# Seven products instead of eight in 34 more weight units, and one unit order on three engines

## The chip, the cores and the metric

One Trainium2 chip; the kernel uses one core of it. The metric is device time in microseconds (us) of one execution, lower is better. A profiled execution gives a trace: what every engine did and when. TensorE is written PE, VectorE DVE, ScalarE ACT, and the queue of SyncE, which issues nearly all transfers, SP.

## The reference

One block of a streaming encoder on x of 256 x 2048 (float32), with 2048-wide projections and a hidden size of 5632:

```python
x = x + 0.5 * swiglu(rms_norm(x, g1), w_gate, w_up, w_down)      # FFN 1: 2048 -> 5632 -> 2048
proj = rms_norm(x, g2) @ w_in                                    # 2048 -> 4112, split into u, q, k, v, g, a
y = concat(pool_mixer(u), gla_mixer(q, k, v, g, a))              # small mixers, 256 x 2048
x = x + y @ w_out
x = x + mem_cross_attention(rms_norm(x, g3), rms_norm(mem, g4))  # w_q, w_kv, 4 heads, w_o
x = x + 0.5 * swiglu(rms_norm(x, g5), w_gate2, w_up2, w_down2)   # FFN 2
out = rms_norm(x, g6)

def swiglu(h, w_gate, w_up, w_down):
    return (silu(h @ w_gate) * (h @ w_up)) @ w_down
```

With 256 rows against some 400 MB of weights the work is a long chain of matrix products in which each weight is used once.

## The kernel before

**Units.** All weights come as a stream of units of 1 MB, a tile `raw` of 128 x 2048 float32, in one order written out by the program (class `Stream`). A float32 product is made of three products in the fast float32 form: a weight is split into a high part `wh` (an ACT copy that rounds) and a low part `wl = raw - wh` (a DVE subtraction), activations are kept as a high and a low part too (`xs`, `ys`), and PE adds up high x high, high x low, low x high (`products`, line 291). While PE works on unit u, unit u+2 is split (`AHEAD = 2`, rings of three `wh` and `wl`) and unit u+5 is loaded (`RAW = 3`, a load is issued when the split that frees its tile is done). `Stream.emit` writes this out; `st.op(f, n)` puts other work n units later. The language then lets a scheduler choose each engine's order from a timing model of its own; every engine runs its queue in the order chosen.

**Groups.** A group is two or four 256 x 512 outputs summed over the depth. In `block_t` a unit holds two depth tiles (k) by 1024 columns: 24 matmuls of 512 columns. `block_a` (transposed outputs, line 276) and `block_b` serve the mixer and the attention and are not changed.

**Seven products.** `block_s` treats some units (`pairs`) as a 2 x 2 by 2 x 2 block product in the Strassen-Winograd form: seven products instead of eight, so 21 matmuls instead of 24 (`seven`, line 388). For that DVE makes four sums of the weight blocks (`add_weights`, lines 347 to 351, tile `T`), which are split like a weight (`split_seven`: `wh<-T`, `wl<-T`, and the three raw blocks that are used as they are, `xh`, `xl`). Sums of the activation blocks are made once by `part_sums` and kept in `xe`. A group with sevens needs four PSUM tiles of two banks each, which is all of PSUM: two hold parts (`a`, `b`) that belong to several outputs, two (`c`, `d`) hold the outputs themselves, on which the plain units (`unit_p`) add up as well. When the last seven is done, `combine` (lines 430 to 435) turns the parts into four tiles of corrections; at the group's end `join` (line 439) adds them to `c` and `d` and passes the sum to the group's own eviction.

Before the change sevens are used in 18 of the 20 gate and up groups of the two FFNs that are 1024 columns wide, in units 0, 2 and 4 of eight: 54 units. The first gate group of each FFN is a `block_t`.

**The order of the groups.** An FFN is cut into parts of 4, 4 and 3 blocks of 512 hidden columns. A part of 4 is gate, up, gate, up, then the down product in two groups of eight units (`into_x`, which adds the result to x rows fetched from and stored to memory). The part of 3 is gate, up, then one group `both` with 512 columns of gate and of up, then down in two groups of six units, in FFN 2 by `down_end`. The hidden activations reach `ys` through `turn` (PE transposes, line 678, then a split), one unit into the down product for those made last. `w_out` and `w_o` are two groups each through `into_x`. After the last down group, and after `w_out` and `w_o`, `fold` turns the new x into `xs`. `mem_in` and `mem_norm` (loading and normalising `mem`) lie in the `w_out` product.

Of the kernel before, what the change touches and what calls it, by code (L numbers as in the profile page):

```python
# [33 lines left out]
class Stream:  # L34
# [30 lines left out]
    def emit(self, load, prepare, split):  # L65
        done, w, late = -1, {}, []
        for u, f in self.items:
# [22 lines left out]
            f(*w.pop(u))  # L90


def build(ctx, tc, I, out):
# [122 lines left out]

    def split(hi, lo, src):
        nc.scalar.copy(hi, src)  # L218
        nc.vector.tensor_tensor(out=lo, in0=src, in1=f32(hi), op=ALU.subtract)  # L219
# [34 lines left out]
    def block_a(srcs, act, evict, delays=(0, 1)):  # L254
# [4 lines left out]
        def unit(gi):  # L259
            def fn(wh, wl):  # L260
# [3 lines left out]
                for kk in range(4):  # L264
# [3 lines left out]
                    for n in range(4):  # L268
# [6 lines left out]
                        for i, (o, w, x) in enumerate(parts):  # L275
                            nc.tensor.matmul(  # L276
                                o, w, x, start=k == 0 and i == 0, stop=last and i == 1
                            )
# [7 lines left out]
    def products(ps, act, k, h, wh, wl, first, last):  # L286

        tok = slice(h * P, (h + 1) * P)
        parts = [(act[:, k, 0, tok], wh), (act[:, k, 0, tok], wl), (act[:, k, 1, tok], wh)]
        for i, (a, w) in enumerate(parts):  # L290
            nc.tensor.matmul(ps, a, w, start=first and i == 0, stop=last and i == 2)  # L291
# [33 lines left out]
    def part_sums(act, ext, i, g):  # L325

        t = scope["pool"].tile([P, 4 * NB], F32, tag="T", name=uid("T"))
        a = t[:, :NB].rearrange("p (k s) -> p k s", k=2)
        e = t[:, NB : 2 * NB].rearrange("p (n s) -> p n s", n=4)
        nc.vector.tensor_tensor(  # L330
            out=a, in0=f32(act[:, 2 * g : 2 * g + 2, 0, :]), in1=f32(act[:, 2 * g : 2 * g + 2, 1, :]),
            op=ALU.add,
        )
        a11, a21, a12, a22 = (a[:, k, h * P : (h + 1) * P] for k in range(2) for h in range(2))
        nc.vector.tensor_tensor(out=e[:, 3], in0=a11, in1=a21, op=ALU.subtract)
        nc.vector.tensor_tensor(out=e[:, 1], in0=a22, in1=a21, op=ALU.subtract)
        nc.vector.scalar_tensor_tensor(
            out=e[:, 2], in0=e[:, 1], scalar=-1.0, in1=a11, op0=ALU.mult, op1=ALU.subtract
        )
        nc.vector.tensor_tensor(out=e[:, 0], in0=a12, in1=e[:, 2], op=ALU.add)  # L340
        split(ext[:, i, 0], ext[:, i, 1], e)
# [12 lines left out]
    def split_seven(u, raw, t):  # L354
# [4 lines left out]
        split(th, tl, t)  # L359
        parts = [x.rearrange("p (b n) -> p b n", n=NB) for x in (th, tl)]  # L360

        if True:
            r = [
                scope["pool"].tile([P, 3 * NB], F32R, tag=n, name=f"{n}{u}", bufs=2)
                for n in ("xh", "xl")
            ]
            split(*r, raw[:, NB:])
            parts.extend(x.rearrange("p (b n) -> p b n", n=NB) for x in r)
# [3 lines left out]
    def seven(banks, act, ext, i, g, first, later, weights):  # L372
# [3 lines left out]
        n4, n1, s2, s3 = ([ext[:, i, p, n] for p in range(2)] for n in range(4))  # L376
# [6 lines left out]
        order = ("P1", "P7", "P5", "P6", "P2", "P3", "P4") if first else (  # L383
            "P1", "P2", "P3", "P7", "P5", "P6", "P4")
        for n in order:
            (a, b), wh, wl = table[n]
            for j, (x, w) in enumerate(((a, wh), (a, wl), (b, wh))):
                nc.tensor.matmul(  # L388
                    banks[n], x, w, start=first and j == 0,
                    stop=not later and n in ("P1", "P5", "P6", "P7") and j == 2,  # L390
                )

    def block_s(srcs, act, ext, pairs, evict, delays=(0, 0)):

        held, n = {}, len(srcs)

        def open_banks():
            a, b, c, d = (ptile(uid("pt")) for _ in range(4))
            held["ps"] = (d, c)
            held["parts"] = (a, b)  # L400
            held["banks"] = {
                "P1": a[:, 0], "P6": a[:, 1], "P7": b[:, 0], "P5": b[:, 1],
                "P2": c[:, 0], "P4": c[:, 1], "P3": d[:, 0],
            }

        def unit_s(g):
            def fn(weights):
                if g == pairs[0]:
                    open_banks()
                seven(held["banks"], act, ext, pairs.index(g), g, g == pairs[0], g != pairs[-1],  # L410
                      weights)
            return fn

        def unit_p(g):
            def fn(wh, wl):
                wh, wl = (w.rearrange("p (k j n) -> p k j n", j=2, n=NB) for w in (wh, wl))
                for j in (1, 0):
                    for h in range(2):
                        for kk in range(2):

                            fresh = (j, h) == (0, 1) and g == min(set(range(n)) - set(pairs)) and kk == 0
                            products(held["ps"][j][:, h, :], act, 2 * g + kk, h, wh[:, kk, j],
                                     wl[:, kk, j], fresh, g == n - 1 and kk == 1)
            return fn

        def combine():
# [17 lines left out]
        for g, src in enumerate(srcs):  # L444
            if g in pairs:
                st.unit(src, unit_s(g), split_seven, add_weights)
                if g == pairs[-1]:
                    st.op(combine)
            else:
                st.unit(src, unit_p(g))  # L450
        for j in (1, 0):
            st.op(lambda j=j: join(j), delays[j])
# [138 lines left out]
    def residual(scale, b):  # L591

        def evict(j, ps):
# [4 lines left out]
            if j:  # L598
                store_x(b)
        return evict  # L600

# [15 lines left out]
    def into_x(w, act, scale, gain=None, k0=0, nk=KT, spread_too=True, src=None):  # L617
# [14 lines left out]
    PAIRS = (0, 2, 4)  # L632

    def pair_sums(g, delay):
        def f():
            if g == PAIRS[0]:
                rows["xe"] = scope["pool"].tile(
                    [P, len(PAIRS), 2, 4, P], F32R, tag="xe", name=uid("xe")
                )
            part_sums(xs, rows["xe"], PAIRS.index(g), g)  # L640
        st.op(f, delay)

    class Ext:


        def __getitem__(self, i):
            return rows["xe"][i]

    def ffn(wg, wu, wd, down):
        gate = {}  # L650

# [30 lines left out]

        for lo, n in FF_PARTS:
            for b in range(0, n - 1, 2):
                n0 = (lo + b) * NB
                if lo == b == 0:
                    block_t(wwide(wg, n0), xs, lambda j, ps: ev_gate(j, ps, 1))
                else:
                    block_s(wwide(wg, n0), xs, Ext(), PAIRS, lambda j, c: ev_gate(j, c, 0))
                block_s(wwide(wu, n0), xs, Ext(), PAIRS, ev_up)  # L690
                held = {}
                st.op(lambda held=held: held.update(gate))
                wait = PAIRS[-1] + 2 if b + 2 < n - 1 else 1
                for j in range(2):
                    st.op(lambda j=j, b=b, held=held: turn(held[j], 4 * (b + j)), wait)
            if n % 2:
                def both(j, ps):
                    if j:
                        ev_up(0, ps)
                    else:  # L700
                        ev_gate(0, ps, 1)
                block_t(wtwo(wg, wu, (lo + n - 1) * NB), xs, both)
                st.op(lambda n=n: turn(gate[0], 4 * (n - 1)), 1)
            down(wd, 4 * lo, 4 * n, lo + n == FF // NB)
# [10 lines left out]
    def down_first(wd, k0, nk, last):  # L715
        into_x(wd, ys, 0.5, G_MIX if last else None, k0, nk, src=None if k0 else I["x"][0])

    for g in PAIRS:
        pair_sums(g, 5)
# [577 lines left out]
```

## Time and profile before

| | |
|---|---|
| time of three runs | 2136.23, 2138.67, 2139.88 us, median 2138.67 us |
| the profiled execution | 2138.64 us |
| its span, first to last instruction | 2136.9 us; 1.7 us lie around it |
| mean granted TensorE clock | 0.998 |
| matmuls and weight loads on PE | 10032 each |
| moved by DMA | 435.92 MB, mean 204 GB/s |

A row of the groups names line, engine and operation, output<-inputs with their shapes, and how often; then total busy us and mean ns of one; then the idle time of the engine just before them and what ended it. PEld is the weight load, which runs beside the matmuls. The ends of matmuls are modelled and overlap, so the pace of matmuls is read from starts, not from their lengths.

### The profile page before, as it was taken

The numbers are of one execution on the slowest core, as the hardware profiler recorded it, in microseconds if no ns is written. First come the engines' busy times: TensorE is split into PE (matmuls) and PEld (weight loads), VectorE is DVE, ScalarE is ACT, GpSimd is POOL, SyncE is SP. The second block draws the span as 40 slices with busy tenths as digits, with TensorE's granted clock in tenths as the row PEclk, the third lists the DMA queues.
The fourth block names the chain that finished last, engine by engine and source line by source line (L and its number), as shares of the span: only waits on it lengthen the run. The fifth ranks groups of instructions, "written<-read, shape, count | busy, mean of one in ns | idle before, by whom it ended". The sixth has DMA issues, their size and how long they took to land.

```text
span 2136.9 us, 24071 instructions
## 1 busy us (share of the span) xinstructions
PE 2115.0 (99%) x10032; PEld 1769.1 (83%) x10032; DVE 1425.8 (67%) x1189; ACT 1006.0 (47%) x890; POOL 14.2 (1%) x41
## 2 busy tenths in 40 slices
PE   9999999999999999999999999999999999999998
PEld 7888887888888888888888888888888887888886
DVE  8786588856765576565666454567874788658744
ACT  7454354534444545455445443455443445434433
POOL 0000000000000000000000000000000000000001
PEclk9999999999999999999999999999999999999999
DMA  7556665666656655557655555666566655766663
GB/s 277 197 197 237 217 214 177 207 230 216 215 197 238 216 161 181 172 173 281 220 189 162 168 168 173 196 202 207 186 236 217 204 200 189 244 210 213 236 217 118
DMA packets 143317, 435.92 MB, mean 204 GB/s; under 512 B 9828, under 2 KB 13000, under 8 KB 142824
## 3 DMA queue, kind: packets, MB, share of 16 engines
q1 hardware_dynamic: 143176, 434.38, 60.1%
q8 instruction: 78, 1.28, 0.2%
q14 instruction: 31, 0.25, 0.0%
q10 hardware_dynamic: 32, 0.01, 0.0%
HBM read 417.58 MB, written 16.78 MB: 203 GB/s over the span
## 4 chain that ended last, share of the span: by engine, by line
PE 97%; DVE 2%; ACT 1%; issue 0%; DMA 0%; SPq 0%; DVEq 0%; ACTq 0%
PE pt L291 58%; PE pa L276 15%; PE pt L388 12%; PE pb L291 6%; PE pe L291 3%; ACT wh L218 1%; PE ph L678 1%; DVE wl L219 1%; PE pl L1071 1%; PE pv L1106 1%; PE px L608 0%; DMA x<-in_x 0%; PE px L562 0%; PE po L941 0%; DVE sg L439 0%
## 5 line engine op out<-in xcount | busy, mean ns | idle before, releaser
L219 DVE TENSOR_TENSOR wl<-raw,wh 128x2048 fp32r<-128x2048 f32 (+2 forms) x328 | 739.8, 2258 | 515.5 <-ACT wh L218 515.1
L218 ACT CAST wh<-raw 128x2048 fp32r<-128x2048 f32 (+2 forms) x329 | 618.4, 1881 | 626.3 <-PE pt L291 415.4
L291 PE MATMUL pt<-wh,xs 128*128 128x512 f32 x1952 | 620.1, 390 | 1.7 <-ACT wh L218 1.7
L291 PE MATMUL pt<-wh,ys 128*128 128x512 f32 x1728 | 534.5, 389 | 0.0
L291 PEld LDWEIGHTS pt<-wh,xs 128*128 128x128 f32 x1952 | 366.4, 188 | 78.1 <-ACT wh L218 2.5
L291 PE MATMUL pt<-wl,xs 128*128 128x512 f32 x976 | 380.4, 390 | 0.0
L291 PEld LDWEIGHTS pt<-wh,ys 128*128 128x128 f32 x1728 | 324.1, 188 | 66.8
L291 PE MATMUL pt<-wl,ys 128*128 128x512 f32 x864 | 336.3, 389 | 0.0
L276 PE MATMUL pa<-xs,wh 128*128 128x512 f32 x896 | 318.6, 399 | 2.1 <-DVE t L250 1.7
L276 PE MATMUL pa<-xs,wl 128*128 128x256 f32 x896 | 249.4, 281 | 0.0
L291 PEld LDWEIGHTS pt<-wl,xs 128*128 128x128 f32 x976 | 183.5, 188 | 37.9
L276 PEld LDWEIGHTS pa<-xs,wh 128*128 128x128 f32 x896 | 168.4, 189 | 41.6 <-issue 2.0
L291 PEld LDWEIGHTS pt<-wl,ys 128*128 128x128 f32 x864 | 162.2, 188 | 33.6
L218 ACT CAST wh<-T 128x2048 fp32r<-128x2048 f32 x54 | 103.1, 1909 | 171.1 <-DVE T L351 162.7
L219 DVE TENSOR_TENSOR wl<-T,wh 128x2048 fp32r<-128x2048 f32 x54 | 123.8, 2293 | 86.4 <-ACT wh L218 86.0
L276 PEld LDWEIGHTS pa<-xs,wl 128*128 128x128 f32 x896 | 169.9, 190 | 1.6 <-issue 0.2
L218 ACT CAST xh<-raw 128x1536 fp32r<-128x1536 f32 x54 | 80.1, 1483 | 98.6 <-DMA raw<-in_ffn_w_gate 36.6
L291 PE MATMUL pb<-wh,xs 128*128 128x512 f32 x384 | 121.7, 392 | 0.5 <-DVE ys L211 0.5
L388 PE MATMUL pt<-wh,xe 128*128 128x512 f32 x324 | 109.5, 390 | 0.8 <-DVE ys L219 0.7
L219 DVE TENSOR_TENSOR xl<-raw,xh 128x1536 fp32r<-128x1536 f32 x54 | 94.8, 1755 | 15.8 <-ACT xh L218 15.5
L291 PEld LDWEIGHTS pb<-wh,xs 128*128 128x128 f32 x384 | 72.1, 188 | 15.6 <-DVE ys L211 0.7
L388 PE MATMUL pt<-xh,xs 128*128 128x512 f32 x216 | 79.5, 391 | 0.9 <-DVE ys L219 0.9
(202 smaller groups left out, 1666.2 us busy)
## 6 DMA issues: line engine op xcount, KB each, us to landing
raw<-in_ffn_w_down SPq DMA_DIRECT2D x88, 1024.0 KB, 5.4
raw<-in_ffn_w_up SPq DMA_DIRECT2D x80, 1024.0 KB, 5.0
raw<-in_ffn_w_gate SPq DMA_DIRECT2D x77, 1024.0 KB, 5.1
raw<-in_w_in SPq DMA_DIRECT2D x32, 1024.0 KB, 5.1
raw<-in_xattn_w_kv SPq DMA_DIRECT2D x32, 1024.0 KB, 5.3
raw<-in_w_out SPq DMA_DIRECT2D x16, 1024.0 KB, 6.1
raw<-in_xattn_w_q SPq DMA_DIRECT2D x16, 1024.0 KB, 5.1
raw<-in_xattn_w_o SPq DMA_DIRECT2D x16, 1024.0 KB, 5.5
```

Of the source, the lines that this page charges most:

```text
L218: nc.scalar.copy(hi, src)
L219: nc.vector.tensor_tensor(out=lo, in0=src, in1=f32(hi), op=ALU.subtract)
L276: nc.tensor.matmul(o, w, x, start=k == 0 and i == 0, stop=last and i == 1)
L291: nc.tensor.matmul(ps, a, w, start=first and i == 0, stop=last and i == 2)
L388: nc.tensor.matmul(banks[n], x, w, start=first and j == 0, stop=not later and n in ("P1", "P5", "P6", "P7") and j == 2,)
L678: nc.tensor.transpose(v[:, i, h * P : (h + 1) * P], g[:, h, i * P : (i + 1) * P], ident)
L1071: nc.tensor.matmul(ps[:, t, :M], ys[:, 4 * h + d, a, tok], xa["K"][:, d, b, :], start=i == 0, stop=i == 11,)
L1106: nc.tensor.matmul(ps[:, d, :S], xa["V"][:, m, a, col], xa["PT"][:, m, b, :], start=i == 0, stop=i == 5,)
```

## The change

- The group `both`, all groups of `into_x` (down in FFN 1 and the first two down products of FFN 2, `w_out`, `w_o`) become `block_s`: three sevens in each of the 2 `both` groups, two in each of the 14 groups of `into_x`. That is 34 units more, 88 in all. `down_end` stays.
- For `into_x`, `combine` passes its result at once to `early_parts`, which adds the corrections to x; `join` then adds `c` and `d` to x with the old `residual`.
- `part_sums` becomes `Sums.make`: three of the four sums lie in a smaller tile, the fourth is written over the block of `xs` or `ys` that no seven reads. For `ys` it is made one and two units into the down product.
- The order of the units in a group changes: pairs 0, 1, 4 in the order 0, 2, 1, 3, 4, ... for gate and up; 2, 3, 4, 0, 5, 1, 6, 7 and others for `into_x`.
- The raw blocks of a seven are split before its sums. Splits stay in the order of the units on ACT and on DVE (`in_turn`), and a unit's matmuls come after those of the unit before (`in_order`).
- `w_out` and `w_o` get scopes of SBUF of their own; `mem_in` and `mem_norm` move behind `w_out`, into the `w_q` product. In the part of 3 the first `turn` comes six units later instead of one.

```diff
+    def in_order():
+        return tc.issue_after(latest["tensor"].ins) if "tensor" in latest else nullcontext()
+
+    def in_turn(engine, f):
+        if engine in latest:
+            with tc.issue_after(latest[engine].ins):
+                latest[engine] = f()
+        else:
+            latest[engine] = f()
+
+    def split_weights(hi, lo, src):
+        in_turn("scalar", lambda: nc.scalar.copy(hi, src))
+        in_turn("vector", lambda: nc.vector.tensor_tensor(
+            out=lo, in0=src, in1=f32(hi), op=ALU.subtract
+        ))
...
+        def make(self, g):
...
+            nc.vector.tensor_tensor(
+                out=a.rearrange("p (k s) -> p k s", k=2), in0=f32(act[:, k, 0, :]),
+                in1=f32(act[:, k, 1, :]), op=ALU.add,
+            )
+            b = a.rearrange("p (n s) -> p n s", n=4)
+            nc.vector.tensor_tensor(
+                out=e[:, 0:2], in0=b[:, 0:4:3], in1=b[:, 1:2].to_broadcast([P, 2, P]), op=ALU.subtract
+            )
+            nc.vector.scalar_tensor_tensor(
+                out=e[:, 2], in0=e[:, 1], scalar=-1.0, in1=b[:, 0], op0=ALU.mult, op1=ALU.subtract
+            )
+            nc.vector.tensor_tensor(out=e[:, 3], in0=b[:, 2], in1=e[:, 2], op=ALU.add)
+            split(self.tile[:, i, 0], self.tile[:, i, 1], e[:, 1:4])
+            split(act[:, 2 * g, 0, P:], act[:, 2 * g, 1, P:], e[:, 0])
...
-        split(th, tl, t)
...
-            split(*r, raw[:, NB:])
+        split_weights(*r, raw[:, NB:])
+        split_weights(th, tl, t)
...
+            if merge is not None:
+                merge(e[:, 2:4], e[:, 0:2])
 
         def join(j):
+            if merge is not None:
+                evict(j, held["ps"][j])
+                return
...
+    def early_parts(scale, b):
+        def merge(minus, plus):
+            for j, e, s in ((1, plus, scale), (0, minus, -scale)):
+                x = x_cols((2 * b + j) * NB, NB)
+                nc.vector.scalar_tensor_tensor(
+                    out=x, in0=e, scalar=s, in1=x, op0=ALU.mult, op1=ALU.add
+                )
+        return merge
...
-            block_t(wwide(w, b * 2 * NB, k0, nk), act, residual(scale, b))
+            block_s(wwide(w, b * 2 * NB, k0, nk), act, sums, orders[b], residual(scale, b, 0),
+                    early_parts(scale, b))
...
-    PAIRS = (0, 2, 4)
+    PAIRS, Y_PAIRS = (0, 1, 4), (0, 1)
+    ORDER = (0, 2, 1, 3, 4, 5, 6, 7)
+    Y_FIRST = (2, 3, 4, 0, 5, 1, 6, 7)
+    O_FIRST = (2, 3, 4, 5, 0, 6, 1, 7)
+    Y_ORDER = (2, 3, 0, 4, 1, 5, 6, 7)
+    CLEAR = 6
...
-                block_t(wtwo(wg, wu, (lo + n - 1) * NB), xs, both)
+                block_s(wtwo(wu, wg, (lo + n - 1) * NB), xs, x_sums, ORDER, both)
...
+            if not end:
+                for i, g in enumerate(Y_PAIRS):
+                    st.op(lambda g=g: y_sums.make(g), 1 + i)
```

More of the change, by code (lines that the diff above doesn't have):

```diff
@@ L290, in products @@
         for i, (a, w) in enumerate(parts):
-            nc.tensor.matmul(ps, a, w, start=first and i == 0, stop=last and i == 2)
+            latest["tensor"] = nc.tensor.matmul(
+                ps, a, w, start=first and i == 0, stop=last and i == 2
+            )
     def block_t(srcs, act, evict, delays=(0, 0)):
@@ L315, in block_t, with jtile @@
             st.op(lambda j=j: evict(j, held["ps"][j]), delays[j])
[L325 to L341, printed above, removed]
+    def jtile():
+        return tmp.tile([P, NB], F32, tag="j", name=uid("j"), bufs=2)
@@ L1004, in build, with out_product @@
     st.op(close_scope, 1)
+    def out_product(name, w, gain, spread_too):
+        sums = Sums("ye", ys, Y_PAIRS)
+        st.op(open_scope(name), 1)
+        for g in Y_PAIRS:
+            st.op(lambda g=g: sums.make(g), 1)
+        into_x(w, ys, 1.0, gain, spread_too=spread_too, sums=sums, orders=y_orders(KT, O_FIRST))
+        st.op(close_scope, 1)
+    out_product("s_out", I["w_out"][0], G_X, True)
     st.op(open_scope("s_x"), 1)
```

176 lines of the change are left out of this document (100 added, 76 removed).

## The prediction

> **What bounds the kernel now.** The page first: the busy times and the chain of waits.
>
> ```profile
> span 2136.9 us, 24071 instructions
> PE 2115.0 (99%) x10032; PEld 1769.1 (83%) x10032; DVE 1425.8 (67%) x1189; ACT 1006.0 (47%) x890; POOL 14.2 (1%) x41
> PE 97%; DVE 2%; ACT 1%; issue 0%; DMA 0%; SPq 0%; DVEq 0%; ACTq 0%
> ```
>
> PE is busy for all but 21.9 us of the span, and the chain that ends last is PE in 97%. So what PE has to stream sets the time, and DVE, at two thirds, is the next in line. A matmul's own price is read from the chain in order of time, around the start of a seven group and of a down product:
>
> ```profile
> 270.27 4.76 PE pt L388 x21
> ...
> 285.23 5.44 PE pt L291 x24
> ...
> 448.56 1.75 PE ph L678 x16
> ```
>
> A seven takes 4.76/21 = 0.2267 us a matmul, a plain unit 5.44/24 = 0.2267. A seven saves 0.68 us of PE.
>
> Then, for DVE, its busy time by stretches (us, PE, PEld, DVE, ACT, POOL): the third seven group of a chain of four; a pair of down groups; `both`; the last down pair of FFN 1; `w_out`; `w_o`.
>
> ```profile
> 353.10:398.10 45.00, 44.10 (x200) 35.82 (x199) 39.26 (x32) 21.84 (x15) 0.00 (x0) 1.00 0.54 187
> ...
> 440.50:529.30 88.80, 88.80 (x402) 73.79 (x401) 52.81 (x34) 35.31 (x20) 0.00 (x0) 1.00 0.63 225
> 612.20:657.50 45.30, 45.30 (x209) 37.73 (x208) 24.64 (x16) 18.50 (x12) 0.00 (x0) 1.00 0.57 203
> 657.50:725.50 68.00, 68.00 (x313) 56.59 (x313) 36.82 (x26) 29.62 (x29) 0.32 (x1) 1.00 0.64 221
> 937.10:1026.00 88.90, 88.90 (x402) 73.80 (x402) 52.06 (x45) 48.26 (x73) 0.00 (x0) 1.00 0.74 260
> 1321.40:1413.10 91.70, 91.70 (x425) 76.65 (x424) 45.84 (x30) 38.46 (x35) 0.00 (x0) 1.00 0.61 194
> ```
>
> Where sevens are made now DVE reaches 39.26/45.00 = 87%; the down groups stand at 52.81/88.80 = 59%. ACT stays near half.
>
> **The change, part by part.**
>
> *PE.* 34 units lose three matmuls each: 102 x 0.2267 = 23.1 us, all of it on the chain of waits. Nothing is added on PE. The Trainium skill, "TensorE: Matmul & The Clock Gate", section "Back-to-back issue gap", gives a sustained 131 ns for a 512-column matmul in a stream of load and matmul pairs and 216 ns for one alone; by 131 ns the change would save 13.4 us. The trace's 227 ns speaks against the 131, and the sum keeps 23.1.
>
> *DVE.* The rows of its groups:
>
> ```profile
> L219 DVE TENSOR_TENSOR wl<-raw,wh 128x2048 fp32r<-128x2048 f32 (+2 forms) x328 | 739.8, 2258 | 515.5 <-ACT wh L218 515.1
> L219 DVE TENSOR_TENSOR wl<-T,wh 128x2048 fp32r<-128x2048 f32 x54 | 123.8, 2293 | 86.4 <-ACT wh L218 86.0
> L219 DVE TENSOR_TENSOR xl<-raw,xh 128x1536 fp32r<-128x1536 f32 x54 | 94.8, 1755 | 15.8 <-ACT xh L218 15.5
> L347 DVE TENSOR_TENSOR T<-raw 128x1024 f32<-128x1024 f32 x54 | 65.9, 1220 | 3.7 <-DMA raw<-in_ffn_w_up 2.2 <-DMA raw<-in_ffn_w_gate 1.2
> L439 DVE TENSOR_TENSOR sg<-pt,sg 128x1024 f32<-128x1024 f32 x36 | 43.9, 1218 | 0.4
> L351 DVE TENSOR_TENSOR T<-T,raw 128x512 f32<-128x512 f32 x54 | 37.1, 686 | 0.7
> L350 DVE TENSOR_TENSOR T<-T,raw 128x512 f32<-128x512 f32 x54 | 36.9, 684 | 0.1
> L595 DVE SCALAR_TENSOR_TENSOR x<-pt,x 128x1024 f32<-128x1024 f32 x28 | 34.1, 1220 | 0.6
> L211 DVE SCALAR_TENSOR_TENSOR xs<-px,gains,xs 128x256 fp32r<-128x256 f32 x64 | 29.0, 479 | 2.1 <-ACT xs L210 1.5
> L668 DVE SCALAR_TENSOR_TENSOR sg<-sg,Rcol,sg 128x512 f32<-128x512 f32 x40 | 27.6, 744 | 0.0
> ...
> L432 DVE TENSOR_TENSOR sg<-pt,sg 128x1024 f32<-128x1024 f32 x18 | 22.0, 1221 | 0.3
> ...
> L1026 DVE TENSOR_SCALAR mem<-mem,Rm 128x2048 f32<-128x2048 f32 x2 | 2.5, 1284 | 0.0
> ...
> L337 DVE SCALAR_TENSOR_TENSOR T<-T 128x128 f32<-128x128 f32 x6 | 1.7, 286 | 0.0
> ```
>
> - A seven costs 2.293 + 1.755 + 1.220 + 0.686 + 0.684 = 6.64 us, a plain unit 2.26: 4.38 more, four operations more.
> - `combine`: two of 512 columns and one of 1024, 2 x 0.69 + 1.22 = 2.59. It is new in 16 groups.
> - `early_parts`: two shaped like L595, 2.44, in 14 groups. `join` costs nothing there (the old residual stays); in `both` it adds 2 x 1.22.
> - `Sums.make`: one of 512 columns (0.69), one of 256 (0.48), two of 128 (0.57), a split of 384 (between 0.48 and 0.69, taken as 0.58) and one of 128 (0.29): 2.6. New for `ys`, two in each of 7 products; for `xs` it stands about where it stood.
>
> Operations that follow each other directly overlap:
>
> ```profile
> 441.80 2.73 DVE L668 SCALAR_TENSOR_TENSOR sg<-sg,Rcol,sg 128x512 f32<-128x512 f32 x4
> ...
> 450.74 2.36 DVE L219 TENSOR_TENSOR ys<-ph,ys 128x1024 fp32r<-128x1024 f32 x2 [0.40 <-ACT ys L218]
> ...
> 466.13 2.29 DVE L219 TENSOR_TENSOR wl<-raw,wh 128x2048 fp32r<-128x2048 f32 x1 [3.15 <-ACT wh L218]
> ```
>
> Four of 0.744 take 2.73, so 0.08 each is to be taken off. A down pair gains 4 x 4.38 + 2 x 2.59 + 2 x 2.44 + 2 x 2.6 = 32.8 us in 38 operations, less 3.0: 29.8. DVE work against what PE then needs (four sevens, 2.7 us less):
> - FFN down pair: 52.8 + 29.8 = 82.6 in 86.1 us, 96%. There are four.
> - last down pair of FFN 1, with the joins of `both` (2.3): 68.9 in 65.3 us, 106%.
> - `w_out`, less the two L1026 of `mem_norm`, which move: 79.3 in 86.2, 92%.
> - `w_o`: 75.6 in 89.0, 85%. `both`: 24.6 + 3 x 4.06 + 2.35 = 39.2 in 43.3, 90%.
>
> Over the whole span DVE goes to some 1425.8 + 34 x 4.06 + 16 x 2.35 + 14 x 2.28 + 14 x 2.1 + 4.6 = 1667 us, 79% of the new span. It fits on the whole; the down groups have nothing left to give, and the lead there is short: in plain stretches DVE idles 3.15 us of each 5.44 for a ring slot that PE frees, so it can't run further ahead than two units.
>
> The tightest place is the start of an FFN down product. From the end of the last up group to the sixth unit (the second seven) PE takes 3 x 5.44 + 1.75 + 4.76 + 5.44 = 28.3 us. DVE has by then to do two joins (2.44), the four gate products (2.73), two `turn` splits (2.36), two plain splits (4.52), two sevens (13.28) and two sums (5.2): 30.5, less 26 x 0.08 = 28.4. The first join can start some 1 us early, when its half is done. It fits by 0.9 us if DVE never waits; the rows at this place show 0.40 and more of waiting for ACT. I take 1.5 us of PE stall per pair, 6 for four, with bounds of 0 and 6 each (the second from the first rival). For the pair at 106%, 3.6 us over: 4. `w_out` 1, `w_o` and `both` 1 together. Sum 12.
>
> *The order of splits and units.* What stalls PE now for late splits:
>
> ```profile
> 362.15 1.48 ACT L218 CAST xh<-raw 128x1536 fp32r<-128x1536 f32 x1 [10.60 <-PE pt L388]
> ...
> 374.62 2.29 DVE L219 TENSOR_TENSOR wl<-T,wh 128x2048 fp32r<-128x2048 f32 x1 [2.05 <-ACT wh L218]
> ...
> PEld pt L388 <- DVE ys L219: 3.2, 4, 1.2
> PEld pt L291 <- ACT wh L218: 2.5, 2, 1.3
> ```
>
> At 362 us ACT stood 10.6 us before an `xh` of a later seven, whose slot PE had yet to free, while the split that PE needed next was queued behind it. In the order of the units this can't arise, and with the raw blocks first the subtraction of `xl` lies in the 2.05 us in which DVE now waits for ACT's copy of the sums. PE's waits for split weights are 3.2 + 2.5 = 5.7 us; I take 4 of it back, bounds 0 and 5.7. A wait in this order has its price: behind an ACT copy that waits for a ring slot or for `T` stand all later splits, and then PE. Where they are late, PE can no longer slip a plain unit in between (second rival).
>
> *Without a price.* ACT gains 34 `xh` of 1.48 us, 50 us, and 44 shorter operations; it stands idle for 1131 us. `mem_in`'s two loads and `mem_norm` move past the `w_out` loads on SP into the `w_q` product, where PE has 16 units of cover; uncovered, the L1026 pair alone would cost 2.6 us. The stores of x follow the group's last eviction as before, with as many transfers on SP. In the part of 3 the first `turn` six units later still lies inside `both`.
>
> Sum, against the profiled execution (2138.64 us, which is the median of the three runs, 2138.67, within 0.03): 2138.6 - 23.1 + 12 - 4 = 2123.5 us.
>
> The Trainium skill, "Perfetto Trace Analysis", section "Tensor Engine Instruction", says that ACT and DVE are strict FIFO queues; it speaks against a fixed order on two nearly full engines. The trace agrees with it in the 10.60 us row, and the time by it would be the first rival's.
>
> **The rivals.**
>
> 1. *DVE becomes the bound in the down groups.* At 353 us, the stretch in which PE waits for splits, DVE got to 87% only. If it can work at no more than 90% where it is pressed, each FFN pair takes 82.6/0.9 = 91.8 us, 5.7 over; the last pair of FFN 1 76.6, 11.3 over; `w_out` 88.1, 1.9 over; `both` 0.3 each. That is 36.6 us lost: 2138.6 - 23.1 + 36.6 = 2152 us, slower than before. It decides from 92% down (there the loss is about 22 us). Against it: much of the idle at 353 us is the 2 us waits for ACT that the new order fills.
>
> 2. *PE, kept to the order, stands at the starts of groups.* Now it fills a late join with plain matmuls:
>
> ```profile
> 354.82 3.17 PE pt L388 x14
> 357.99 2.72 PE pt L291 x12
> 360.71 1.37 PE pt L388 x6
> ```
>
> Here 12 plain matmuls ran inside a seven. A stall like that stretch's 45.00 - 44.10 = 0.9 us at each of the 14 starts of a seven group behind a seven group is 12.6 us, beside the forecast's terms: 2136 us.
>
> 3. *The DVE work hides entirely* and PE keeps only its other waits: 2138.6 - 23.1 - 4 = 2111.5 us.
>
> 4. *The sevens don't save their matmuls* (the scheduler undoes it): PE's count would stay at 10032. The diff leaves no room for that.
>
> **How the numbers follow.** Forecast 0.50; rival 1 0.18; rival 2 0.18; rival 3 0.12; rival 4 0.02. The likeliest gives 2123.5 us. The range takes in rival 3 with 1.5 us for the jitter of the runs, 2110, and reaches into rival 1 as far as 2147, where DVE works at 91%; left out is less than half of rival 1 and little else. About 0.2%, 4.3 us, is what a measurement of this kernel tells from no change. Faster by more: the forecast, rival 3 and half of rival 2, 0.71; within: the rest of rival 2, a little of rival 1 and rival 4, 0.12; slower: rival 1, 0.17.
>
> **What would show it.** PE must count 10032 - 102 = 9930 matmuls, at 0.227 us from start to start. DVE's busy time should be near 1667 us, and 80 to 85 us in each FFN down pair. Right: PE's waits for `wl<-T`, `xl` and `ys` lie at the first sevens of the down products and sum to about 12 us; the 10.6 us stand of ACT is gone. Wrong: the chain of waits turns from PE to DVE over whole down groups (rival 1), PE stands before P3 at group starts (rival 2), or a queue waits for x or `mem` where I saw cover.

## The result: slower by 2.4%, and the profile after

| | before | after |
|---|---|---|
| median | 2138.50 us of four runs (2136.23 to 2139.88) | 2190.15 us of four runs (2188.16 to 2190.62) |
| ratio to before | | 1.0241, 95% interval 1.0229 to 1.0253 |
| the profiled execution | 2138.64 us, span 2136.9 us | 2189.99 us, span 2188.2 us |
| mean granted clock | 0.998 | 0.987 |
| matmuls | 10032 | 9930 |

The forecast was 2123.5 us. The first lines of the page after, the same three that open the prediction:

```profile
span 2188.2 us, 24316 instructions
PE 2115.6 (97%) x9930; PEld 1760.0 (80%) x9930; DVE 1655.6 (76%) x1489; ACT 1066.5 (49%) x974; POOL 15.2 (1%) x41
PE 67%; DVE 22%; issue 6%; ACT 4%; DMA 0%; ACTq 0%; DVEq 0%; SPq 0%
```

The 102 matmuls are gone, and DVE's total (1655.6 us) is close to the 1667 forecast. Yet PE's busy time is where it was (2115.6 against 2115.0 us), though it does less, and the chain of waits has passed from PE alone (97%) to PE 67%, DVE 22%. The two things behind that are the waits of PE and the granted clock. The waits of PE's weight loads (us in total, times, longest):

```profile
PEld pt L312 <- ACT ys L239: 16.3, 5, 3.8
PEld pt L312 <- DVE ys L240: 15.7, 5, 3.6
PEld pt L429 <- DVE wl L234: 12.6, 16, 1.7
PEld pt L429 <- DVE sg L499: 6.8, 2, 3.4
```

In the new line numbers 312 is a plain product, 429 a seven, 234 and 240 are subtractions of weights and activations, 239 a copy of activations, 499 is `join`. The largest two rows are a wait that the prediction had only at the first sevens: here plain units (line 312) wait for `ys`, the hidden activations themselves.

**Where the time went.** With the first matmul of each group as its border, each group's length can be set against its length before. Added up over the span the changes give the 51.3 us by which the span grew; against what each group was to save (1.4 us for two sevens, 2.0 for three, 23.1 in all) the loss is about 74 us:

| groups | change of length, us | loss against the saving |
|---|---|---|
| first down groups of the four 8-unit down products | +8.1, +7.8, +7.6, +7.6 | 36.7 |
| second down groups of these | -1.4 each | 0 |
| the group of sevens ahead of each of these down products | +3.1, +4.0, -0.4, +4.6 | 11.3 |
| last down product of FFN 1, and the mixer's first group behind it | +1.6, -1.1, +6.8 | 10.1 |
| first and second groups of `w_out` and `w_o` | -1.4, +3.8; -1.4, +3.0 | 9.6 |
| `both`, twice | -0.4, -0.1 | 3.5 |
| other groups | -0.6 to +1.2 each | about 3.4 in sum |

**One of the four.** The chain of waits from the end of the up group (184.7 us) to the first seven of the down product (start, us, what):

```profile
183.64 1.22 DVE sg L499
184.86 1.13 DVE T L391
...
187.04 1.40 DVE sg L733 x2
188.44 0.60 DVE T L394
189.05 2.20 DVE wl L234
191.25 1.33 DVE sg L733 x2
192.57 1.67 DVE xl L234
194.25 0.61 DVE T L395
...
194.96 1.92 ACT wh L233
...
199.11 2.29 DVE wl L234
201.40 1.14 DVE T L391
202.53 1.67 DVE xl L234
204.20 1.15 DVE ys L240
...
205.39 7.04 PE pt L312 x20
```

Line 733 is the gate product that finishes the last hidden activations; 391, 394 and 395 are the sums of the weight blocks for the sevens to come. Between the two halves of the gate product stand a sum (394) for a seven that PE reaches 14 us later at the earliest, and the split (234) of the third unit's weights, due 8 us later. The same place before, in the timeline of DVE:

```profile
180.18 2.51 DVE L439 TENSOR_TENSOR sg<-pt,sg 128x1024 f32<-128x1024 f32 x2
182.61 2.73 DVE L668 SCALAR_TENSOR_TENSOR sg<-sg,Rcol,sg 128x512 f32<-128x512 f32 x4
...
191.55 2.36 DVE L219 TENSOR_TENSOR ys<-ph,ys 128x1024 fp32r<-128x1024 f32 x2 [0.40 <-ACT ys L218]
```

Before, join, gate products, done: from the end of the up group (181.3 us) to the last gate product took 4.0 us, now 7.8. On PE the transposes of these products came at 189.2 us before, 7.9 us after the end of the up group, and come at 195.6 now, 10.9 after it (the timelines of PE, before and after):

```profile
189.21 1.91 PE L678 MATMUL ph<-ident,sg 128*128 128x128 f32 x16
```

```profile
195.61 1.91 PE L743 MATMUL ph<-ident,sg 128*128 128x128 f32 x16
```

Then ACT, in its timeline after (the bracket is the idle time ahead and what ended it):

```profile
194.96 1.92 ACT L233 CAST wh<-T 128x2048 fp32r<-128x2048 f32 x1 [6.73 <-DVE T L395]
...
199.94 1.92 ACT L239 CAST ys<-ph 128x1024 fp32r<-128x1024 f32 x2
```

The transposes are done at 197.5 us, but the copy of `ys` stands behind a copy of `T`, for which ACT waited 6.73 us, and two more splits. The subtraction of `ys` on DVE stands behind sums and splits too, until 204.2 us. PE needs this `ys` in its third unit. The timeline of PE, and then its stretches (the columns as in the prediction; the third number from the end is the granted clock):

```profile
201.00 0.80 PE L312 MATMUL pt<-wh,ys 128*128 128x512 f32 x1 [3.48 <-ACT ys L239]
...
205.39 1.22 PE L312 MATMUL pt<-wh,ys 128*128 128x512 f32 x2 [2.32 <-DVE ys L240]
```

```profile
197.20:201.00 3.80, 0.32 (x3) 0.08 (x2) 3.80 (x2) 3.80 (x4) 0.00 (x0) 0.85 0.97 379
201.00:205.40 4.40, 2.08 (x5) 1.17 (x5) 4.40 (x5) 0.86 (x1) 0.00 (x0) 0.50 0.89 315
205.40:210.00 4.60, 4.60 (x11) 3.64 (x12) 2.36 (x3) 0.00 (x0) 0.00 (x0) 0.50 0.26 65
210.00:215.00 5.00, 5.00 (x24) 4.10 (x23) 0.55 (x1) 1.91 (x1) 0.00 (x0) 0.99 0.42 171
```

PE stands 3.5 and 2.3 us. And it comes back at half its clock: from 205.4 to 210 us PE counts as fully busy and does 11 matmuls in 4.6 us, where the next 5 us hold 24. Some 15 matmuls at about 0.43 instead of 0.227 us are 3.0 us more. 3.5 + 2.3 + 3.0 is 8.8 of the 9.5 us that this group loses. (Four of these matmuls lie between the two waits; at full clock they would have been done 0.8 us sooner and the second wait would have been that much longer.)

Apart from one at the very end of each trace, the trace after has ten such stretches at half clock, of 3.4, 6.8 or 10.2 us, 51.2 us in all; that of before has one of 3.4 us. In "TensorE: Matmul & The Clock Gate", section "What's actually happening", the Trainium skill says that the clock falls to half after an idle window of about 3.4 us and comes back after as much work. The trace agrees on the length of the stretches, not on the length of the wait. With a mean clock of 0.85 over 197.2 to 201.0 us and half clock from then on, the clock fell at about 199.9 us, 2.4 us after the transposes ended. Some 55 us earlier a wait of 2.26 us was followed by half clock 1 us after PE had gone on (timeline of PE, and the stretch):

```profile
144.22 0.50 PE L429 MATMUL pt<-xh,xs 128*128 128x512 f32 x1 [2.26 <-DVE ys L240]
145.20:148.60 3.40, 3.40 (x9) 2.63 (x9) 2.41 (x7) 3.27 (x5) 0.00 (x0) 0.51 0.25 43
```

A wait of 2.37 us at 747.5 us left the clock at 1.00, so the length of one wait does not settle it.

### The profile page after: what moved, and what is told of

Same layout as the page of the kernel before. It is cut to its first block, busy times and chain, and to the rows that moved or that the text cites. A ratio compares the mean times of both kernels' runs of the same rounds, so it can differ in the third digit from the quotient of the medians.

```text
span 2188.2 us, 24316 instructions
## 1 busy us (share of the span) xinstructions
PE 2115.6 (97%) x9930; PEld 1760.0 (80%) x9930; DVE 1655.6 (76%) x1489; ACT 1066.5 (49%) x974; POOL 15.2 (1%) x41
## 4 chain that ended last, share of the span: by engine, by line
PE 67%; DVE 22%; issue 6%; ACT 4%; DMA 0%; ACTq 0%; DVEq 0%; SPq 0%
PE pt L312 30%; PE pa L297 14%; PE pt L429 11%; DVE wl L234 8%; PE pb L312 6%; ACT wh L233 4%; DVE xl L234 4%; PE pe L312 3%; DVE T L391 2%; DVE sg L499 1%; DVE T L395 1%; DVE T L394 1%; DVE sg L733 1%; PE pl L1159 1%; PE pv L1194 1%
## 5 line engine op out<-in xcount | busy, mean ns | idle before, releaser
L234 DVE TENSOR_TENSOR wl<-raw,wh 128x2048 fp32r<-128x2048 f32 (+2 forms) x294 | 660.7, 2251 | 266.5 <-ACT wh L233 266.2
L233 ACT CAST wh<-raw 128x2048 fp32r<-128x2048 f32 (+2 forms) x294 | 551.0, 1881 | 370.1 <-PE pt L312 125.9
L312 PE MATMUL pt<-wh,xs 128*128 128x512 f32 x1856 | 589.7, 391 | 0.0
L312 PE MATMUL pt<-wh,ys 128*128 128x512 f32 x1280 | 410.0, 397 | 29.1 <-ACT ys L239 15.1
L233 ACT CAST wh<-T 128x2048 fp32r<-128x2048 f32 x88 | 168.2, 1911 | 432.8 <-DVE T L395 384.4
L234 DVE TENSOR_TENSOR wl<-T,wh 128x2048 fp32r<-128x2048 f32 x88 | 201.6, 2291 | 160.5 <-ACT wh L233 160.5
L312 PEld LDWEIGHTS pt<-wh,ys 128*128 128x128 f32 x1280 | 244.4, 192 | 84.5 <-ACT ys L239 16.3
L312 PE MATMUL pt<-wl,ys 128*128 128x512 f32 x640 | 253.2, 396 | 4.0 <-DVE wl L234 4.0
L234 DVE TENSOR_TENSOR xl<-raw,xh 128x1536 fp32r<-128x1536 f32 x88 | 154.0, 1749 | 0.0
L391 DVE TENSOR_TENSOR T<-raw 128x1024 f32<-128x1024 f32 x88 | 107.1, 1217 | 1.8 <-DMA raw<-in_ffn_w_gate 0.7
L429 PE MATMUL pt<-wh,xs 128*128 128x512 f32 x240 | 94.7, 395 | 0.0
```

The costliest lines, as they stand in the source:

```text
L233: in_turn("scalar", lambda: nc.scalar.copy(hi, src))
L234: in_turn("vector", lambda: nc.vector.tensor_tensor(out=lo, in0=src, in1=f32(hi), op=ALU.subtract))
L312: latest["tensor"] = nc.tensor.matmul(ps, a, w, start=first and i == 0, stop=last and i == 2)
L391: nc.vector.tensor_tensor(out=v[:, 0:2], in0=w[:, 1:3], in1=w[:, 0:1].to_broadcast([P, 2, NB]), op=ALU.add)
L429: latest["tensor"] = nc.tensor.matmul(banks[n], x, w, start=n in fresh and j == 0, stop=n in ends and j == 2)
```

## The experiments

The theory after the trace: **order, not load**. DVE has time for the whole of the work, but at the end of an up group the scheduler lets sums and splits for later sevens go ahead of the chain join, gate product, transpose, `ys`, on which PE's third unit hangs. The rivals: the two orders that the change fixes (`in_order`, `in_turn`) hold things up; the new order of the units alone does; DVE simply has too much to do (rival 1 of the prediction).

**The two orders, one at a time and together.** PE free:

```diff
-            with in_order():
-                f(*w.pop(u))
+            f(*w.pop(u))
```

> The changed kernel with PE's unit order taken away (in_order); splits stay in order. Theory A (at the start of a down product DVE makes the seven's sums ahead of the gate products, so the last hidden activations, which the third unit needs, come late): PE can pull a later unit forward only in part, 2175 to 2188 us. Rival B (the fixed orders themselves cost the time): most of the loss goes with PE's order, under 2160 us.

Splits free:

```diff
-        if engine in latest:
-            with tc.issue_after(latest[engine].ins):
-                latest[engine] = f()
-        else:
-            latest[engine] = f()
+        latest[engine] = f()
```

> The changed kernel with the order of splits on ACT and DVE taken away (in_turn); PE's unit order stays. Theory A: the sums of the weights are not in that order anyway, 2170 to 2200 us. Rival B: under 2160 us, as the 10 us stands of ACT before copies of the sums go.

Both edits:

> The changed kernel with neither order: the 34 more sevens, the sums in the down groups and the unit sequences alone. Theory A: still slower than before by over 20 us, 2160 to 2190 us. Rival B: the 23 us of matmuls saved show, 2115 to 2130 us.

Measured: 2193.55 us (1.0262 of before, 1.0245 to 1.0279), 2190.16 us (1.0250, 1.0235 to 1.0266), and with both free 2172.80 us (1.0166, 1.0151 to 1.0181). Taking away either order alone brings nothing back (the first run lies above the 2175 to 2188 us expected); taking away both brings back 17 us. But with both free the first down groups are still 7.0, 6.9, 6.4 and 7.4 us longer than before: this largest loss has another cause. What comes back lies in the groups ahead of the down products (+0.6, +0.1, -0.3, +0.9) and in the second `w_out` group (-0.2, less two matmuls of `w_q` that ran inside it). Why it takes both, no run shows.

**The two orders in the kernel before**, with the raw blocks of a seven split first and no other part of the change:

```diff
-            f(*w.pop(u))
+            with in_order():
+                f(*w.pop(u))
...
-        split(th, tl, t)
...
-            split(*r, raw[:, NB:])
+            split_weights(*r, raw[:, NB:])
+            split_weights(th, tl, t)
```

> The kernel before with both orders alone (units in order on PE, splits in order on ACT and DVE, raw blocks of a seven split first); 54 sevens as before. Theory A: the orders cost little, 2134 to 2145 us. Rival B: 2155 to 2190 us.

Measured: 2135.99 us of ten runs, 0.9991 (0.9982 to 1.0001). At most a small gain, inside the noise, and no loss in the kernel before. The third groups of sevens, in which ACT stood 10.6 us, became 1.7 us shorter each, as the prediction had it; in the whole it is 1.6 us against the runs of before beside it (2137.57), not 4.

**Unit 4 later.** In the change the third unit of a down product is unit 4, which reads the last `ys`:

```diff
-    Y_FIRST = (2, 3, 4, 0, 5, 1, 6, 7)
+    Y_FIRST = (2, 3, 0, 1, 4, 5, 6, 7)
```

> The changed kernel with the first down group of an FFN in the order 2, 3, 0, 1, 4, 5, 6, 7 instead of 2, 3, 4, 0, 5, 1, 6, 7, so that the unit that needs the last hidden activations is the fifth and not the third. Theory A (those activations come late because sums stand ahead of the gate products on DVE): the waits for ys go, some 5 us of the 9 us lost in each of four groups, 2165 to 2178 us. Rival C (DVE has too much to do in these groups, whatever the order): the loss turns into waits for split sevens, 2185 to 2200 us.

Measured: 2180.76 us, 1.0189 (1.0162 to 1.0216), between the two expected ranges. Three of the four first groups fall from +7.6 and more to +2.2 or +2.3, so the wait for `ys` was theirs; the one in FFN 2 that comes first stays at +7.2, and the second group of the last down product of FFN 1 grows by 7.7 us. PE's largest waits are now for split weights:

```profile
PEld pt L312 <- DVE wl L234: 19.4, 13, 2.6
PEld pt L429 <- DVE wl L234: 18.1, 20, 2.1
```

Moving the demand trades one late thing for another; DVE's order is as it was. Why the one group in FFN 2 did not follow, no run shows.

**The order in DVE's queue.** The sums of weights and of activations may not pass the last gate product; the work is the same:

```diff
+    def after_up():
+        return tc.issue_after(latest["up"].ins) if "up" in latest else nullcontext()
...
+        with after_up():
+            nc.vector.tensor_tensor(
+                out=v[:, 0:2], in0=w[:, 1:3], in1=w[:, 0:1].to_broadcast([P, 2, NB]), op=ALU.add
+            )
...
-                nc.vector.scalar_tensor_tensor(
+                latest["up"] = nc.vector.scalar_tensor_tensor(
```

(the first operation of `Sums.make` stands under `after_up` too)

> The changed kernel; DVE's sums of weights and of activations are kept behind the last gate product issued before them, in DVE's queue. Theory A: the gate products end some 4 us earlier, the transposes and ys with them, and 4 to 7 us come back in each of four groups: 2160 to 2175 us. Rival C: what is won at ys is lost at the first seven, 2185 to 2195 us.

Measured: 2157.87 us, 1.0094 (1.0072 to 1.0115): 32 us back from this edit, more than expected. That is net; the first group of the last down product of FFN 1 goes from +1.6 to +8.1 us, the second group of `w_out` from +3.8 to +6.5. The timeline of DVE at the same place (join is now L505, the gate product L739, the `ys` subtraction L244, the first sum L397):

```profile
182.21 2.51 DVE L505 TENSOR_TENSOR sg<-pt,sg 128x1024 f32<-128x1024 f32 x2
184.63 2.73 DVE L739 SCALAR_TENSOR_TENSOR sg<-sg,Rcol,sg 128x512 f32<-128x512 f32 x4
187.28 1.22 DVE L397 TENSOR_TENSOR T<-raw 128x1024 f32<-128x1024 f32 x1
...
193.82 1.22 DVE L244 TENSOR_TENSOR ys<-ph,ys 128x1024 fp32r<-128x1024 f32 x1
...
195.76 1.22 DVE L244 TENSOR_TENSOR ys<-ph,ys 128x1024 fp32r<-128x1024 f32 x1
```

Join and gate products run as before the change, `ys` is done at 197.0 us instead of 206.5, and all four first down groups are now 1.3 to 1.4 us shorter than before: the whole of what two sevens save. So in these groups it was the order, at the same work. The stretch of the second down pair says too that it was not the load:

```profile
443.80:529.90 86.10, 86.10 (x390) 71.50 (x389) 75.75 (x68) 41.22 (x30) 0.00 (x0) 1.00 0.65 230
```

DVE is busy for 75.75 of 86.10 us, 88%, and PE never stands.

**Less load instead.** The first down groups of the FFNs as plain products, with the sums of `ys` two units later:

```diff
+            if orders[b] is None:
+                block_t(wwide(w, b * 2 * NB, k0, nk), act, residual(scale, b))
+            else:
+                block_s(...)
...
-    Y_FIRST = (2, 3, 4, 0, 5, 1, 6, 7)
+    Y_FIRST = None
```

> The changed kernel with eight products, in the old order, in the first of the two groups of each FFN down product and of w_out and w_o (14 sevens fewer); their sums are made two units later. Theory A and rival C both: the 8 us lost in each of four FFN groups go, w_out and w_o give up 1.4 us each: 2150 to 2162 us. If the time stays over 2180 us, both are wrong and the loss lies elsewhere.

`w_out` and `w_o` kept their sevens, since their first groups have an order of their own; so 10 sevens fewer (9960 matmuls), not the 14 of that text. Measured: 2152.02 us, 1.0062 (1.0043 to 1.0082). The first down groups are as long as before the change. It buys that by giving up ten sevens, 6.8 us of PE, that the run above kept, and it changes load and order together, so it does not tell them apart. It is still 5.9 us faster than the run above; in its trace the last down product of FFN 1 has its two groups at 0.0 and -1.4 us (the second keeps its sevens), against +8.1 and -1.1.

**The new order of the units alone**, in the kernel before, with plain products:

```diff
-        for gi, src in enumerate(srcs):
-            st.unit(src, unit(gi))
+        for gi in order:
+            st.unit(srcs[gi], unit(gi))
...
+        return [g for g in (2, 3, 4, 0, 5, 1, 6, 7) if g < nk // 2]
```

> The kernel before with nothing but the first down group of each FFN part in the order 2, 3, 4, 0, 5, 1, 6, 7; no more sevens. Theory A (the order alone leaves the hidden activations just in time, it takes the sums as well): 2138 to 2146 us. Rival D (the third unit comes too early for its activations whatever DVE does): 2160 us and more.

Measured: 2136.61 us of ten runs, 0.9995 (0.9985 to 1.0004). The order alone costs nothing.

**The second join.** In the groups ahead of the down products something is still lost with the sums behind the gate product (+0.9, +3.5, -0.7, +4.2 us). The timeline of DVE in that run shows why:

```profile
395.97 1.22 DVE L505 TENSOR_TENSOR sg<-pt,sg 128x1024 f32<-128x1024 f32 x1
397.10 2.28 DVE L238 TENSOR_TENSOR wl<-raw,wh 128x2048 fp32r<-128x2048 f32 x1
399.30 1.22 DVE L397 TENSOR_TENSOR T<-raw 128x1024 f32<-128x1024 f32 x1
400.44 1.75 DVE L238 TENSOR_TENSOR xl<-raw,xh 128x1536 fp32r<-128x1536 f32 x1
402.11 1.22 DVE L244 TENSOR_TENSOR ys<-ph,ys 128x1024 fp32r<-128x1024 f32 x1
403.24 1.22 DVE L505 TENSOR_TENSOR sg<-pt,sg 128x1024 f32<-128x1024 f32 x1
```

The second of the two joins comes 7.3 us after the first, behind a split, a sum, `xl` and a `ys`. Joins and `ys` splits free PSUM tiles, which come from one ring of four. PE's third product starts here when the `ys` is done, at the same place in FFN 2 when the join is (1830.09 us, after 2.47 us of waiting):

```profile
403.38 0.80 PE L435 MATMUL pt<-xh,xs 128*128 128x512 f32 x1 [2.60 <-DVE ys L244]
```

The edit makes the later sums and splits follow the join:

```diff
-            nc.vector.tensor_tensor(
+            latest["up"] = latest["vector"] = nc.vector.tensor_tensor(
```

> The kernel with the sums behind the gate products, and besides: the splits and the sums that are issued after a group's join stay behind that join in DVE's queue. In the kernel before it the second join stood behind a split, sums, xl and a split of ys, and PE stood some 3 us before the third product (P3) of the fourth seven group of a part. Theory E (the late join is that loss): the three such groups get back 1 to 4 us each, 2145 to 2152 us. Rival F (DVE is simply full there; kept behind the join, the splits come late instead): 2155 to 2165 us.

Measured: 2151.93 us, 1.0060 (1.0046 to 1.0073). In its trace the join stands at 398.70 us, 4.5 us after the first, ahead of `xl`, and these groups are at -0.8, +0.2, -0.7 and +0.9 us, about 8 us less in all. The profiled execution is the fastest of its four, that of the run before the slowest of its four; the intervals of the two runs just touch, so the gain in time (5.9 us by the medians) is likely rather than sure. The second groups of `w_out` and `w_o` fall too, from +6.5 and +3.0 to +3.8 and +1.4 us, with all their sevens.

```profile
398.70 1.22 DVE L505 TENSOR_TENSOR sg<-pt,sg 128x1024 f32<-128x1024 f32 x1
```

**The pressed places.** What remains lies where the prediction had DVE at 85 to 106%: the second groups of `w_out` and `w_o`, and the last down product of FFN 1. In the trace after, around the start of the second `w_out` group:

```profile
1003.00:1031.00 28.00, 26.39 (x124) 21.45 (x122) 25.01 (x24) 15.87 (x21) 0.00 (x0) 1.00 0.80 279
```

DVE is busy for 25.01 of 28.00 us, 89%, and PE stands 1.6 us: 0.8 for a `combine` and 0.8 for a split, with 2.3 us more for splits just behind this stretch. Ahead of the mixer, in the same trace, DVE is not full: it stands 5.45 us for PE's last seven before it can `combine`, at the end of the group, and behind that `combine` come splits and corrections, and only then the `xs` that PE waits for (timelines of DVE and PE):

```profile
746.37 1.22 DVE L487 TENSOR_TENSOR sg<-pt,sg 128x1024 f32<-128x1024 f32 x1 [5.45 <-PE pt L429]
...
765.95 0.50 PE L297 MATMUL pa<-xs,wh 128*128 128x512 f32 x1 [3.21 <-DVE xs L212]
```

From the version with the sums behind the gate product, these groups lose their eight sevens (and the fourth sum of `w_out` and `w_o` gets a tile of its own, since plain units now read the block that it was written over):

```diff
+            if orders[b] is None:
+                block_t(wwide(w, b * 2 * NB, k0, nk), act, residual(scale, b))
...
+                sums=sums, orders=[None, None] if last else y_orders(nk, Y_FIRST))
...
+        into_x(w, ys, 1.0, gain, spread_too=spread_too, sums=sums, orders=[list(O_FIRST), None])
```

> The kernel with the sums behind the gate products, but eight products again in the two groups of the last down product of FFN 1 and in the second group of w_out and of w_o (8 sevens fewer). Rival C in its narrow form (in these groups, and only there, DVE has more to do than fits): the 8.1 + 8.1 - 1.1 us around the last down product and the 6.5 + 3.0 us of the second groups go, 2130 to 2138 us. If the loss were a fixed delay of something else in the mixer or the attention, it would stay: 2150 us or more.

Measured: 2138.07 us of ten runs, 0.9999 (0.9990 to 1.0008): level with before. The last down product of FFN 1, the mixer behind it and the second groups of `w_out` and `w_o` are back at their lengths before, to 0.0 us. 20 us came back net, though the eight sevens are 5.4 us of matmuls more. The run shows where the loss was. It does not show that the load made it: with the eight sevens go their sums and their late `combine` too, and the run with the second join had already brought part of it back by order alone.

**Both edits**, the join first and the eight sevens fewer:

> Both edits together: 26 sevens more than the kernel before, sums behind gate products, splits behind joins. If the losses found so far are all there is, 26 x 0.68 = 17.7 us of matmuls come through but for some 2 us in the two groups of gate and up: 2119 to 2126 us, faster than both kernels. If Rival F holds, 2130 us and more.

Measured: 2130.17 us of five runs (2129.40 to 2133.46), 0.9962 (0.9949 to 0.9976), faster than the kernel before and than the change. That is outside the 2119 to 2126 us expected. The number alone would fit Rival F, but the groups ahead of the down products are at -0.8, +0.2, -0.7 and +0.9 us, so the splits behind the joins are not late there.

78 matmuls fewer than before (9954) are worth 17.7 us; 7.7 are measured against the runs of before beside it (2137.91). Its profiled execution, the slowest of the five, has 6.8 us at half clock; the largest losses in it are 5.2 us in `w_q` and 3.5 in the two `both`.

**What is left of it.** In that trace the first `w_q` group is 5.2 us longer than before the change, and PE waits there for an `xs`. On ACT an operation of `mem_norm` stands before the load of `mem`, ahead of two copies to `xs`:

```profile
1036.53 0.42 ACT L253 ACTIVATE j<-mem 128x256 f32<-128x256 f32 x1 [3.35 <-DMA mem<-in_mem]
```

```diff
-    st.op(mem_in, 2)
-    st.op(mem_norm, 6)
+    st.op(mem_in, 5)
+    st.op(mem_norm, 12)
```

> The version with both repairs (2130.17 us, 0.9962 of before), with mem_in 5 instead of 2 units and mem_norm 12 instead of 6 units into the w_q product; nothing is left out. In that version's trace PE stands 3.7 us in w_q's first group before an xs that DVE writes (the group is 5.2 us longer than before the change), and on ACT an activation of mem_norm waits 3.35 us for the load of mem, ahead of two copies to xs. Theory 1 (the move of mem_in and mem_norm is the cause: ACT's queue stands before the transfer): with both later the xs copies come first, w_q's first group falls back to about 24.6 us, and the time falls by about 5 us to about 2125 us, 0.994 of before. Theory 2 (the fold of x itself is late, because the corrections of w_out's first group push it back): the wait for xs stays and the time does not move (2129 to 2132 us). A third way: mem_norm's eight activations and the two scalings of mem now come late in w_q and are late for the K and V product, up to 5 us given back there.

Measured: 2131.14 us of six runs (2128.40 to 2133.76), 0.9966 (0.9953 to 0.9978): no gain. The time is where Theory 2 had it, but Theory 1 was not tested: the activation still stands ahead of the copies, after a shorter wait:

```profile
1033.62 0.42 ACT L253 ACTIVATE j<-mem 128x256 f32<-128x256 f32 x1 [1.99 <-DMA mem<-in_mem]
```

The group is 2.5 us longer than before instead of 5.2 in the profiled executions, but the one is the slowest of its five runs and the other the second fastest of its six. Whether `mem` is what holds `w_q` stays open.

## Why the prediction was wrong, step by step

- **PE, 23.1 us: right.** There are 9930 matmuls, and where nothing waits, a group with two sevens is 1.4 us shorter (the second down groups, the first groups of `w_out` and `w_o`), twice 0.68.
- **DVE's total and its work per pair: right in sum, high by place.** 1655.6 us against 1667. For a down pair 82.6 us were forecast; 75.75 were measured with the sums in order, and in the change itself 72.3 of the 95.2 us that the second pair took. Fewer units' splits fell between the borders (15, where the window before held 16 to 17).
- **The stall of the FFN down pairs, 1.5 us each and 6 in all: this is the step that failed.** They cost 9.5, 9.2, 9.0 and 9.0 us, 36.7. The prediction named the right place, the start of the down product, and the right list of DVE's work, 28.4 us of it. But it compared that sum with the time to the sixth unit, as if DVE took the work in the order in which PE needs it. There is an earlier deadline inside: the third unit, unit 4, needs the last `ys`, and PE transposes for it 7.9 us after the end of the up group (in the trace before). The scheduler put a sum and a split between the gate products, and four sums and five splits in all ahead of the `ys`, of which one split alone was due by then. With the same work in the right order (the sums behind the gate products) the stall is zero.
- **The clock was not priced.** Half clock stretches rose from 3.4 to 51.2 us. With matmuls every 0.43 instead of 0.227 us that is at most about 23 to 24 us of loss. PE's busy time gives the same: it is 0.6 us longer where 102 matmuls fewer should have made it 23.1 shorter, so slower matmuls took 23.7 us more.
- **The pair at 106% (4 us), `w_out` (1), `w_o` and `both` (1): too low.** With the mixer behind it the last down product lost 10.1 us, the second groups of `w_out` and `w_o` 9.6, `both` 3.5. The prediction summed DVE's work over the group; in the mixer's first group (+6.8 us) the price was a `combine` that had to wait for the last seven, and `xs` late behind it, after a lull of DVE. Why `both` keeps at most 0.4 of its 2.0 us in any run was not tried.
- **The orders, 4 us back: right in kind in the kernel before, not in the change.** Alone they gave 1.6 us, inside the noise; in the changed kernel the two together cost 17 us. The 10.6 us stand of ACT, which was to go, came back at the same place as a stand for the sums (timeline of ACT, after), and the group there is 0.2 us shorter, not 1.7:

```profile
373.33 1.91 ACT L233 CAST wh<-T 128x2048 fp32r<-128x2048 f32 x1 [10.37 <-DVE T L395]
```

- **Without a price:** the stores, ACT's 34 `xh`. ACT's total did rise as forecast, to 49%. What counted was where it stood: `ys` was queued behind a copy that waited 6.73 us. The Trainium skill's sentence on strict FIFO queues ("Perfetto Trace Analysis", section "Tensor Engine Instruction") covers this; the prediction applied it to fullness alone.
- **The rivals.** The first is wrong in the four FFN down pairs, to which it gave 22.8 of its 36.6 us: 88% without a wait. That their loss, 36.7 us, equals its sum is chance. For the last down product, `w_out` and `w_o` it stays possible: giving up eight sevens there won 20 us, but load and order went together. The second had the groups ahead of the down products right in kind (PE before a PSUM tile that a late join or `ys` split still holds), 11.3 us in all, in three places, where it had 12.6 us over fourteen. The third and the fourth are refuted.

The terms as measured, by the pages before and after: -23.1 for the matmuls, +50.7 for PE standing (from 21.9 to 72.6 us), +23.7 for slower matmuls give +51.3, the growth of the span.

Still open: why both orders have to be free for the 17 us; and why the last down product of FFN 1 lost more (8.1 us in its first group) with the sums behind the gate product. There the trace shows ACT standing 5.46 us for a sum of activations, ahead of the last copy of `ys` at 672.67 us (its timeline):

```profile
668.47 0.30 ACT L243 CAST ys<-j 128x128 fp32r<-128x128 f32 x1 [5.46 <-DVE j L376]
```

That fits the same mechanism on ACT; no run separates it.

## What to carry to other kernels

Where an engine does work for now and work for later, compare its load with each deadline inside the stretch, and not only with the last one: write down for the first units what PE reads, and which queue entries stand ahead of it on every engine of that chain. If a scheduler chooses the order, tie the work that is not urgent behind the urgent chain before judging the load; here one such tie was worth 32 us at unchanged work. Of savings that load a helper engine, give up those in places where they cost more than they bring: eight sevens fewer, worth 5.4 us, won 20 us, even if their cause was not separated.

## What was not expected of the hardware

A wait of PE can cost more than its length. Within a stand of 3.5 us the granted clock fell to 0.50, and with a second stand of 2.3 us it stayed there for 10.2 us (199.9 to 210.1); one stand of 2.26 us was followed by 3.4 us of it, another of 2.37 us by none. At half clock matmuls start every 0.43 instead of 0.227 us, while PE counts as busy. So a page with PE at 97% hid both: the busy share fell by two points, and the matmuls inside the busy time were slower. Such stretches total 51.2 us after, 37.5 with the sums behind the gate product, 6.8 in the version with both edits.
